# Row sums of a seven-product output projection made by accumulating DMAs instead of GpSimd, and squares of the other half's tokens at other heads

## The chip, the cores and the metric

The kernel runs on one core of a Trainium2 chip. Its engines are TensorE (PE in the profile; PEld is its weight load), VectorE (DVE), ScalarE (ACT), GpSimd (POOL) and SyncE (SP, which here only issues DMAs). Each works through its own queue in order. DMAs are issued from SP's queue (hardware_dynamic) and POOL's (software_dynamic). The metric is the device time of one execution in microseconds (us), as the median of several runs.

## The reference

One decoder layer over 1024 tokens of width 2048, in f32. Two groups of 8 heads share one input projection:

```python
hn = rmsnorm(h, norm_mix_g[i])
proj = hn @ w_in[i]
# heads 0-7: stick-breaking attention (products of 1 - sigmoid in place of a softmax)
# heads 8-15: differential attention (softmax1 - lam * softmax2), with its own RMSNorm
mixed = jnp.concatenate([sb_out * jax.nn.silu(sb_g), df_out * jax.nn.silu(df_g)], axis=-1)
h = h + mixed @ w_out[i]
gate = jax.nn.sigmoid(rmsnorm(h, norm_ple_g[i]) @ w_ple_gate[i])
h = h + gate * (p[i] @ w_ple_proj[i])
return rmsnorm(h, norm_final_g)
```

`mixed` is 1024 x 2048: sixteen head outputs of 128 columns.

## The kernel before, in words

Everything lies transposed: features on the 128 partitions, tokens along the row, reversed and in two halves of 512. Half 1, which holds the earlier tokens, is worked first, then half 0, whose attention also reads the keys and values of half 1. Each f32 matmul is made of three on float32r: every operand is split into a high part (a cast on ACT) and a low part (a difference on DVE), and high x high, high x low and low x high are summed in PSUM (L213 to L215).

**Input projection and attention.** For each half and each head, two units (`unit`) of 96 matmuls give q and k, then v and the gate. Their weights come as four blocks of 512 KB per unit: a load on SP (L150), the cast `whi` on ACT (L151) and the difference `wlo` on DVE (L152), each in two buffers. The attention of a head is a list of steps with due times. A counter goes up after every three matmuls, and a step that is due is put among the matmuls of the next head's units (`Side.tick`). PE's order is therefore written out by hand over the whole kernel. Up to the second output projection below, the other queues are ordered by a planner that simulates the program.

A step of a stick-breaking head: scores on PE, sigmoids on ACT (L304, L305), a running product (L306) and a product (L307) on DVE, transposes on PE (L345), splits (`lead` L350/L351, `awh`/`awl` L357/L358), and the product with v on PE (L373 to L378). DVE's instruction at L554 makes the gate's input and marks the start of each head's attention. The head's output is multiplied into the gate's tile `sg` (three buffers; L387 for stick-breaking, L408 for differential heads) and stored to DRAM as `mixed_d[half, head]` from SP (L389, L410). In half 1, k and v are also stored from POOL's queue; in half 0 they are loaded from there, again by POOL's queue, into `k2` and `v2`, two buffers each.

Half 1 runs heads 0 to 15. Half 0 runs 8 to 15 and then 0, 4, 1, 5, 2, 6, 3, 7.

**Squares.** The norm of the tokens of half 0 needs the sum of squares over 16 row blocks of x. At the ninth head of half 1 (`hd == H`), 16 loads (L585, the `xt` ring of four buffers, held back until the last weight load issued by then), 16 squares on ACT (L105, L109; two buffers `sq`) and 15 additions on POOL (L110) make it. It is used two heads later.

**Output projection.** It is made of two phases, each over eight heads as inner dimension: first heads 8 to 15, then 0 to 7. In each phase the 2 x 2 block product (two halves of tokens, two groups of four heads) takes seven block products in place of eight. With A11 and A12 the two groups of half 1, A21 and A22 those of half 0, the row sums are S1 = A21 + A22, S2 = S1 - A11, S3 = A21 - A11 and S4 = A12 - S2. `combine_` makes them, head pair by head pair: four loads of `mixed_d` on SP (L246), four additions or subtractions of 128x512 on POOL (L249 to L252) and four stores to `comb_d` on SP (L254). `combine` is called after a head of half 0 where a pair is complete, eight times in all, the last one in the middle of the first phase; it holds its loads until the last put before it, if there is one. Each sum is later loaded by SP and split by ACT and DVE (`load_operand`).

For the weights, DVE makes differences (`diff`) of four blocks; the fourth, `b22`, goes with S4. `whigh` casts each on ACT (L865) and `wlow` makes the low part on DVE (L876). The results go out through `put`, from POOL's queue: a plain store to `half_d` in the first phase (L746), an accumulating DMA into `h_d` in the second (L744). In this part DVE and ACT are ordered by hand too. The ring of `sg` is used again here for `u2` and `u3` (L965 and following).

After that come the gate's projection and the final norm.

Of the kernel before, what the change touches and what calls it, by code (L numbers as in the profile page):

```python
# [13 lines left out]
F32 = mybir.dt.float32  # L14
F32R = mybir.dt.float32r
BF16 = mybir.dt.bfloat16
AF = mybir.ActivationFunctionType
ALU = mybir.AluOpType
AX = mybir.AxisListType

P = 128
D = 2048
S = 1024
HALF = 512
NK = D // P
H = 8
SB_SCALE = 128.0 ** -0.5
DF_SCALE = 64.0 ** -0.5
ORDER1 = [*range(16)]
ORDER0 = [*range(8, 16), 0, 4, 1, 5, 2, 6, 3, 7]  # L30
EPS = 1e-6
SUB_EPS = 1e-5

# [13 lines left out]
def _body(ctx, nc, tc, ap):  # L47
# [4 lines left out]
    ev = ctx.enter_context(tc.tile_pool(name="ev", bufs=1))  # L52
    pp = ctx.enter_context(tc.tile_pool(name="pp", bufs=2, space=PSUM))
    dram = ctx.enter_context(tc.tile_pool(name="dram", bufs=1, space=bass.MemoryType.DRAM))
    V, G, A, T = nc.vector, nc.gpsimd, nc.scalar, nc.tensor
# [163 lines left out]
    mixed_d = dram.tile([2, NK, P, HALF], F32, name="mixed_d", tag="mixed_d")  # L219

    comb_d = dram.tile([2, 4, 4, P, HALF], F32, name="comb_d", tag="comb_d")
    h_d = dram.tile([2, NK, P, HALF], F32, name="h_d", tag="h_d")
    part_d = dram.tile([8, P, HALF], F32, name="part_d", tag="part_d")
    half_d = dram.tile([2, NK, P, HALF], F32, name="half_d", tag="half_d")
# [4 lines left out]

    KA = [[(8 + i, 12 + i) for i in range(4)], [(i, 4 + i) for i in range(4)]]  # L230

    def combine(ph, i):

        a, b = KA[ph][i]
        if lastput[0] is not None:
            with tc.issue_after(lastput[0].ins):
                return combine_(ph, i, a, b)
        return combine_(ph, i, a, b)

    lastput = [None]  # L240

    def combine_(ph, i, a, b):
        t = []
        for src in (mixed_d[0, a], mixed_d[0, b], mixed_d[1, a], mixed_d[1, b]):
            x = ev.tile([P, HALF], F32, name="cmb", tag="xt", bufs=4)
            nc.sync.dma_start(x, src)  # L246
            t.append(x)
        a21, a22, a11, a12 = t
        G.tensor_tensor(a22, a21, a22, op=ALU.add)  # L249
        G.tensor_tensor(a21, a21, a11, op=ALU.subtract)  # L250
        G.tensor_tensor(a11, a22, a11, op=ALU.subtract)
        G.tensor_tensor(a12, a12, a11, op=ALU.subtract)  # L252
        for j, x in enumerate((a22, a11, a21, a12)):
            nc.sync.dma_start(comb_d[ph, j, i], x)  # L254


    def attention(at, pz, half, hd, q, qz, K, KL, VV, sg, vf):
# [102 lines left out]
        def mix(pr, g):  # L360
            if g == 0:
                avs[pr] = pp.tile([P, 4, P], F32, name="av", tag="t")
            av4 = avs[pr]
            av = av4[:, 2:4, :].rearrange("p a b -> p (a b)")
            for j in range(2):
                blk = 2 * (pr + g) + j
                vv = VV[blk // 4]
                last = blk == nb - 1
                if blk == 2 * pr:


                    for i in range(2):
                        T.matmul(av4[:, 0:2, :], vv[:, i, blk % 4, :], wjs[pr, g][j], start=i == 0, stop=i == 1)  # L373
                    continue
                wh, wl = wjs[pr, g][j]
                T.matmul(av, vv[:, 0, blk % 4, :], wh, start=blk == 2 * pr + 1, stop=False)  # L376
                T.matmul(av, vv[:, 1, blk % 4, :], wh, start=False, stop=False)  # L377
                T.matmul(av, vv[:, 0, blk % 4, :], wl, start=False, stop=last)  # L378
            if not last:
                return  # L380
            ms_ = slice(pr * 2 * P, (pr + 1) * 2 * P)
            sm = ev.tile([P, 2, P], F32, name="sm", tag="sm", bufs=5)
            A.copy(sm[:, 1, :], av4[:, 3, :])
            V.reduce_sum(sm[:, 0, :], av4[:, 0:3, :].rearrange("p a b -> p b a"), axis=AX.X)
            av = sm.rearrange("p a b -> p (a b)")
            if sb:
                V.tensor_tensor(sg[:, ms_], av, sg[:, ms_], op=ALU.mult)  # L387
                if pr == 1:
                    nc.sync.dma_start(mixed_d[half, hd], sg)  # L389
                return  # L390
            sq = ev.tile([P, 2 * P], F32, name="sqv", tag="sm", bufs=5)
            A.activation(sq, av, AF.Square)
            V.scalar_tensor_tensor(sg[:, ms_], av, subg[:, 0:1], sg[:, ms_], op0=ALU.mult, op1=ALU.mult)
            sqh = ev.tile([P, 2 * P], F32R, name="sqh", tag="sm", bufs=5)
            sql = ev.tile([P, 2 * P], F32R, name="sql", tag="sm", bufs=5)
            A.copy(sqh, sq)
            V.tensor_tensor(sql, sq, sqh.bitcast(F32), op=ALU.subtract)
            sqs[pr] = sq, sqh, sql

        def norm(pr):  # L400
            ms_ = slice(pr * 2 * P, (pr + 1) * 2 * P)
            sq, sqh, sql = sqs[pr]
            msq = pp.tile([P, 2 * P], F32, name="msq", tag="t")
            T.matmul(msq, onesr, sqh, start=True, stop=False)
            T.matmul(msq, onesr, sql, start=False, stop=True)
            rs_ = ev.tile([P, 2 * P], F32, name="rsub", tag="sm", bufs=5)
            rstd_from(msq, 1.0, eps5, SUB_EPS, rs_, sq)
            V.tensor_tensor(sg[:, ms_], sg[:, ms_], rs_, op=ALU.mult)  # L408
            if pr == 1:
                nc.sync.dma_start(mixed_d[half, hd], sg)  # L410

        n0 = nb // 2
        n1 = n0 - 1
# [20 lines left out]
    with tc.tile_pool(name="at", bufs=2) as at, tc.tile_pool(name="pz", bufs=2, space=PSUM) as pz:  # L434
# [4 lines left out]
        for half in (1, 0):  # L439
            tsl = slice(half * HALF, half * HALF + HALF)  # L440
            X = {}
            if half == 1:
# [3 lines left out]
                for i in range(8):  # L446
# [4 lines left out]
                    src = ap["xT"].rearrange("(a k p) t -> k p a t", a=2, p=P)[kts[0], :, :, tsl]  # L451
# [9 lines left out]
                    for j in range(2):  # L461
                        kt = kts[j]
                        X[kt] = split_scaled(kt, x2[:, j, :], gvec[:, 0, kt:kt + 1])
                        xs.append(x2[:, j, :])
            else:
                for kt in KT:
                    xt = ev.tile([P, HALF], F32, name="xt", tag="xt", bufs=4)
# [5 lines left out]

            for hd in (ORDER0, ORDER1)[half]:
                sb = hd < H
# [79 lines left out]
                sg = at.tile([P, HALF], F32, name="sg", tag="sg", bufs=3)  # L555
# [20 lines left out]
                    K.append(k2)  # L576
                    VV.append(v2)
                side.add(attention(at, pz, half, hd, q, qz, K, KL, VV, sg, vf))
                if half == 1 and hd == H:
                    pin = lastw[0].ins  # L580
                    ss0 = SumSq(ev, "ssq")
                    for kt in range(NK):
                        xt = ev.tile([P, HALF], F32, name="xs", tag="xt", bufs=4)
                        with tc.issue_after(pin):
                            nc.sync.dma_start(xt, ap["xT"][kt * P:(kt + 1) * P, 0:HALF])  # L585
                        ss0.add(xt)
                if half == 1 and hd == H + 2:
                    rstds[0] = ss0.rstd(ev, "rstd0")
                if half == 0 and hd >= H:
                    for kt in (2 * (hd - H), 2 * (hd - H) + 1):  # L590
                        for hf in range(2):
                            with tc.issue_after(lastw[0].ins):
                                nc.sync.dma_start(h_d[hf, kt], ap["xT"][kt * P:(kt + 1) * P, hf * HALF:hf * HALF + HALF])
                if half == 0 and hd < H and hd:
                    n = ORDER0.index(hd) - H
                    combine(*((0, n - 1) if n < 5 else (1, n - 5)))


        h = {}
# [141 lines left out]
        def put(o, ph, hf, ch):  # L741

            if ph:
                lastput[0] = G.dma_start(h_d[hf, ch], o, accum_op=ALU.add)  # L744
            else:
                lastput[0] = G.dma_start(half_d[hf, ch], o)  # L746

        def ftile():
            return ev.tile([P, HALF], F32, name="hc", tag="f", bufs=4)
# [28 lines left out]
        for u in range(0, 8, 2):  # L778
# [8 lines left out]
            for i in range(2):  # L787
                product(u + i, 0, "A12", aa[i], False, tick=True)
                o = ftile()
# [64 lines left out]
        def whigh():  # L854
            i = len(wmade)
            if i == len(wtodo):
                return
            n, nm, fn = wtodo[i]
            src = fn()
            pool, tag = WRING[i % len(WRING)]  # L860
            if pool == "wp":
                t = wp.tile([P, 2, 4 * P], F32R, name="wpr", tag=tag)
            else:
                t = at.tile([P, 2, 4 * P], F32R, name="wpr", tag=tag, bufs=BUFS.get(tag, 2))
            A.copy(t[:, 0], src)  # L865
            wmade.append((src, t))

        def wlow():
            i = wlate[0]
            if i == len(wtodo):  # L870
                return
            wlate[0] += 1
            n, nm, _ = wtodo[i]
            src, t = wmade[i]
            wmade[i] = None
            V.tensor_tensor(t[:, 1], src, t[:, 0].bitcast(F32), op=ALU.subtract)  # L876
            ph, u = UNITS[n]
            wq[u, ph, nm] = t[:, 0], t[:, 1]
            if nm == "S4":
                wload(n + 2, 22)  # L880
# [61 lines left out]
        for ph in range(2):  # L942
            for u in range(8):
# [6 lines left out]
                if ph:  # L950
                    a = pp.tile([P, HALF], F32, name="pa", tag="acc", bufs=2)
# [6 lines left out]
                if ph == 0 and u % 3 == 2:  # L958
                    b, c = [pp.tile([P, HALF], F32, name="pb", tag="acc", bufs=2) for _ in range(2)]
                else:  # L960
                    bc = pz.tile([P, 2, HALF], F32, name="pbc", tag="z")
                    b, c = bc[:, 0, :], bc[:, 1, :]
# [29 lines left out]
                o = ftile()  # L992
# [4 lines left out]
                if last:  # L997
                    p2()
                prev = u, ph, b, c, s1, u2
                if ph == 0 and u == 1:  # L1000
                    combine(1, 3)
                if ph == 0 and 1 <= u < 5:
                    for nm, i in (("A11", u - 1), ("A12", u - 1)):
                        xq.append((slot[0] + 3, load_operand(1, nm, i)))
        ph = pair("ph", "k", F32R)
# [35 lines left out]
        ss0 = SumSq(ev, "rstd1")  # L1041
# [43 lines left out]
        for pc in range(4):  # L1085
            raw = wp.tile([P, 2, 2, 2, P], F32, name="wraw", tag="wraw", bufs=2)
            nc.sync.dma_start(raw, ap["w_gate"][7][pc])
            for k2 in range(2):
# [3 lines left out]
                else:  # L1092
                    t = pair(f"wz{kk}", H1[kk], F32R, (P, 2, 2, 2, P))
# [5 lines left out]
        for tq in range(2):  # L1099
# [13 lines left out]
            for c in range(2):  # L1113
                t = h[0, 7 + 8 * c][:, ts]
# [72 lines left out]
```

## Time and profile before

| | us |
|---|---|
| median of 3 runs | 2515.78 (2513.76 to 2515.96) |
| the profiled execution | 2510.27 |
| its span, first to last instruction | 2508.5 |
| PE busy | 2441.4 (97%) |
| DVE busy | 1668.4 (67%) |
| ACT busy | 1161.9 (46%) |
| POOL busy | 288.9 (12%) |

The first half of the tokens runs from 0 to about 860 us, the second to about 1765, the first phase of the output projection to about 1930 and the second to 2084, the gate and the end to 2508. A matmul of 512 columns takes some 390 ns in the records, but the next starts some 230 ns after it; busy time of PE is their union.

In a timeline, a line has the start and the duration in us, engine, line of the kernel and operation, what it writes and reads with the shape, and in brackets the idle time of the engine before it and what ended that. In a list of waits, the numbers are the total in us, how many times, and the longest. In a list of DMA issues, the last number is the median time in us from issue to landing.

### The profile page before, as it was taken

To read this page: it belongs to the slowest core of one execution; us is meant where nothing else is said; L and a number is where in the kernel's file an instruction comes from. 1 tells how busy PE (TensorE), PEld (TensorE's weight loads), DVE (VectorE), ACT (ScalarE), POOL (GpSimd) and SP (SyncE) were. 2 spreads that over 40 slices of the span, in tenths; PEclk is the share of its full clock that TensorE was granted. 3 is DMA by queue.
4 is the path that set the end of the run, shared out by engine and by line. 5 is a ranking of instruction groups with operands and counts; after the bars stand their busy time and mean duration, and the time that the engine had idled before them with its cause. 6 is when DMAs were issued, how large, how long until landed. Compare 5 with 4: busy or idle time off the path is not lost.

```text
span 2508.5 us, 31234 instructions
## 1 busy us (share of the span) xinstructions
PE 2441.4 (97%) x11626; PEld 2034.8 (81%) x11626; DVE 1668.4 (67%) x2677; ACT 1161.9 (46%) x1920; POOL 288.9 (12%) x281
## 2 busy tenths in 40 slices
PE   8999999999999999999999999999999998999996
PEld 7888888788887888888887888887787876888886
DVE  6554555777877888888876565667678673547555
ACT  6332333555556655555555333335523224637342
POOL 3000000300000000001111010101021114321112
PEclk9999999999999999999999999999999999999998
DMA  5333333633334333334443333435656786333433
GB/s 189 113 116 116 114 105 125 206 123 118 109 122 164 121 107 122 114 117 143 148 142 126 101 126 94 135 113 183 228 190 217 164 199 211 129 119 115 133 101 101
DMA packets 135415, 346.26 MB, mean 138 GB/s; under 512 B 14496, under 2 KB 18592, under 8 KB 135264
## 3 DMA queue, kind: packets, MB, share of 16 engines
q1 hardware_dynamic: 114096, 288.43, 35.6%
q0 software_dynamic: 21168, 55.85, 7.8%
q8 instruction: 91, 1.49, 0.2%
q14 instruction: 60, 0.49, 0.1%
HBM read 281.31 MB, written 71.30 MB: 141 GB/s over the span
## 4 chain that ended last, share of the span: by engine, by line
PE 87%; DVE 7%; DMA 2%; ACT 2%; issue 1%; SPq 0%; DVEq 0%; ACTq 0%
PE acc L213 20%; PE acc L214 20%; PE acc L215 20%; PE tp L345 2%; PE pbc L756 2%; PE pbc L758 2%; PE pbc L757 2%; DVE st L306 1%; PE z L286 1%; PE z L287 1%; PE av L378 1%; DVE wlo L152 1%; PE av L377 1%; PE av L376 1%; PE pa L758 1%
## 5 line engine op out<-in xcount | busy, mean ns | idle before, releaser
L213 PE MATMUL acc<-xh,whi 128*128 128x512 f32 x2464 | 981.4, 398 | 6.3 <-ACT xh L138 6.3
L214 PE MATMUL acc<-xl,whi 128*128 128x512 f32 x2464 | 963.9, 391 | 0.8 <-DVE xl L139 0.8
L215 PE MATMUL acc<-xh,wlo 128*128 128x512 f32 x2464 | 964.0, 391 | 0.0
L152 DVE TENSOR_TENSOR wlo<-wraw,whi 128x1024 fp32r<-128x1024 f32 (+1 forms) x317 | 398.8, 1258 | 374.5 <-ACT whi L151 369.2
L215 PEld LDWEIGHTS acc<-xh,wlo 128*128 128x128 f32 x2464 | 463.6, 188 | 101.1 <-DVE wlo L152 1.3
L151 ACT CAST whi<-wraw 128x1024 fp32r<-128x1024 f32 (+1 forms) x317 | 333.0, 1051 | 457.2 <-PE acc L214 397.0
L213 PEld LDWEIGHTS acc<-xh,whi 128*128 128x128 f32 x2464 | 464.8, 189 | 93.6 <-ACT xh L138 6.8
L214 PEld LDWEIGHTS acc<-xl,whi 128*128 128x128 f32 x2464 | 464.9, 189 | 88.3 <-DVE xl L139 2.3
L357 ACT CAST awh<-tp 128x256 fp32r<-128x256 f32 (+1 forms) x160 | 80.3, 502 | 180.9 <-PE tp L345 153.5
L358 DVE TENSOR_TENSOR awl<-tp,awh 128x256 fp32r<-128x256 f32 (+1 forms) x160 | 93.1, 582 | 97.9 <-ACT awh L357 96.7
L110 POOL TENSOR_TENSOR ssq<-ssq,sq 128x512 f32<-128x512 f32 x80 | 119.0, 1488 | 326.6 <-ACT sq L109 278.8
L314 ACT ACTIVATE et<-z,mx 128x512 f32<-128x512 f32 (+7 forms) x128 | 94.6, 739 | 53.6 <-DVE mx L311 52.7
L865 ACT CAST wpr<-T 128x512 fp32r<-128x512 f32 x64 | 39.2, 623 | 164.9 <-DVE T L822 164.0
L306 DVE TENSOR_TENSOR_SCAN st<-pt 128x511 f32<-128x511 f32 (+3 forms) x64 | 89.9, 1405 | 20.8 <-ACT pt L304 20.2
L311 DVE TENSOR_REDUCE mx<-z 128x1 f32<-128x512 f32 (+7 forms) x128 | 96.4, 753 | 1.2
L304 ACT ACTIVATE pt<-z 128x512 f32<-128x512 f32 (+3 forms) x64 | 41.6, 650 | 79.7 <-DVE z L293 79.7
L378 PE MATMUL av<-awl,v 128*128 128x256 f32 x256 | 73.4, 287 | 5.2 <-DVE awl L358 5.2
L376 PE MATMUL av<-awh,v 128*128 128x256 f32 x256 | 72.5, 283 | 0.7 <-ACT awh L357 0.7
L377 PE MATMUL av<-awh,v 128*128 128x256 f32 x256 | 72.3, 283 | 0.0
L286 PE MATMUL z<-k,q 128*128 128x512 f32 (+2 forms) x160 | 56.9, 360 | 4.5 <-ACT et L314 4.5
L322 DVE SCALAR_TENSOR_TENSOR et<-et,l 128x512 f32<-128x512 f32 (+3 forms) x64 | 53.0, 829 | 11.8 <-ACT et L321 11.8
L321 ACT ACTIVATE et<-et,l 128x512 f32<-128x512 f32 (+3 forms) x64 | 49.7, 777 | 17.6 <-DVE l L320 17.1
(309 smaller groups left out, 3627.8 us busy)
## 6 DMA issues: line engine op xcount, KB each, us to landing
wraw<-w_in SPq DMA_DIRECT2D x255, 512.0 KB, 3.6
wraw<-w_gate SPq DMA_DIRECT2D x64, 512.0 KB, 3.6
wraw<-w_out SPq DMA_DIRECT2D x56, 256.0 KB, 3.7
k_d<-k POOLq DMA_DIRECT2D x16, 512.0 KB, 3.9
v_d<-v POOLq DMA_DIRECT2D x16, 512.0 KB, 2.9
mixed_d<-sg SPq DMA_DIRECT2D x32, 256.0 KB, 3.1
k<-k_d POOLq DMA_DIRECT2D x16, 512.0 KB, 3.6
v<-v_d POOLq DMA_DIRECT2D x16, 512.0 KB, 4.4
```

The lines of the kernel that those rows point to most:

```text
L110: lastadd[0] = eng.tensor_tensor(self.acc, self.acc, s, op=ALU.add)
L151: A.copy(hi[:, o], raw[:, o])
L152: V.tensor_tensor(lo[:, o], raw[:, o], hi[:, o].bitcast(F32), op=ALU.subtract)
L213: T.matmul(acc[c], hi[:, k2, kh, c, :], xh, start=first, stop=False)
L214: T.matmul(acc[c], hi[:, k2, kh, c, :], xl, start=False, stop=False)
L215: T.matmul(acc[c], lo[:, k2, kh, c, :], xh, start=False, stop=last)
L306: V.tensor_tensor_scan(st[:, off + 1:nkey], pt[:, off:nkey - 1], pt[:, off:nkey - 1], initial=1.0, op0=ALU.mult, op1=ALU.bypass)
L311: V.reduce_max(mx, z[:, vw], axis=AX.X, negate=True)
L314: A.activation(et[:, vw], z[:, vw], AF.Exp, bias=mx[:, 0:1], accum_out=l)
L376: T.matmul(av, vv[:, 0, blk % 4, :], wh, start=blk == 2 * pr + 1, stop=False)
L377: T.matmul(av, vv[:, 1, blk % 4, :], wh, start=False, stop=False)
L378: T.matmul(av, vv[:, 0, blk % 4, :], wl, start=False, stop=last)
```

## The change

`combine` goes. Each head's output is added to the row sums that it is part of as soon as it is there, by a new function `mixed` in place of the store:

- Half 1, a first-group head (A11): `mixed_d` is stored as before; ACT makes a negated copy in a tile of the `xt` ring, and three plain stores on SP put it into S2, S3 and S4.
- Half 1, a second-group head (A12): `mixed_d` as before; the negated copy is added to S4 by one accumulating DMA from POOL's queue.
- Half 0, a first-group head (A21): no store to `mixed_d`; the tile is stored to S1 from SP and added to S3, S2 and S4 by three accumulating DMAs.
- Half 0, a second-group head (A22): `mixed_d` from SP; the tile is added to S1, S2 and S4 by three accumulating DMAs.

S4 so comes out with the opposite sign, and the weights that go with it are negated in their split. Half 0 now runs its stick-breaking heads in the order 0 to 7. The squares are made four blocks at a time at heads 1 to 4 of half 1. The holding of `combine` behind the last put goes with it.

```diff
-ORDER0 = [*range(8, 16), 0, 4, 1, 5, 2, 6, 3, 7]
+ORDER0 = [*range(8, 16), *range(8)]
...
-    def combine_(ph, i, a, b):
-        t = []
-        for src in (mixed_d[0, a], mixed_d[0, b], mixed_d[1, a], mixed_d[1, b]):
-            x = ev.tile([P, HALF], F32, name="cmb", tag="xt", bufs=4)
-            nc.sync.dma_start(x, src)
-            t.append(x)
-        a21, a22, a11, a12 = t
-        G.tensor_tensor(a22, a21, a22, op=ALU.add)
-        G.tensor_tensor(a21, a21, a11, op=ALU.subtract)
-        G.tensor_tensor(a11, a22, a11, op=ALU.subtract)
-        G.tensor_tensor(a12, a12, a11, op=ALU.subtract)
-        for j, x in enumerate((a22, a11, a21, a12)):
-            nc.sync.dma_start(comb_d[ph, j, i], x)
+    def mixed(half, hd, t):
+
+
+        ph, second, i = (0 if hd >= H else 1), hd % H >= 4, hd % 4
+        S1, S2, S3, S4 = [comb_d[ph, j, i] for j in range(4)]
+        if half == 1 or second:
+            nc.sync.dma_start(mixed_d[half, hd], t)
+        if half == 1:
+            n = ev.tile([P, HALF], F32, name="neg", tag="xt", bufs=4)
+            A.activation(n, t, AF.Copy, scale=-1.0)
+            if second:
+                G.dma_start(S4, n, accum_op=ALU.add)
+            else:
+                for d in (S2, S3, S4):
+                    nc.sync.dma_start(d, n)
+            return
+        if second:
+            G.dma_start(S1, t, accum_op=ALU.add)
+        else:
+            nc.sync.dma_start(S1, t)
+            G.dma_start(S3, t, accum_op=ALU.add)
+        G.dma_start(S2, t, accum_op=ALU.add)
+        G.dma_start(S4, t, accum_op=ALU.add)
...
                 if pr == 1:
-                    nc.sync.dma_start(mixed_d[half, hd], sg)
+                    mixed(half, hd, sg)
...
-                if half == 1 and hd == H:
+                if half == 1 and 1 <= hd < 5:
                     pin = lastw[0].ins
-                    ss0 = SumSq(ev, "ssq")
-                    for kt in range(NK):
+                    if hd == 1:
+                        ss0 = SumSq(ev, "ssq")
+                    for kt in range(4 * hd - 4, 4 * hd):
                         xt = ev.tile([P, HALF], F32, name="xs", tag="xt", bufs=4)
                         with tc.issue_after(pin):
                             nc.sync.dma_start(xt, ap["xT"][kt * P:(kt + 1) * P, 0:HALF])
...
-                if half == 0 and hd < H and hd:
-                    n = ORDER0.index(hd) - H
-                    combine(*((0, n - 1) if n < 5 else (1, n - 5)))
...
-            A.copy(t[:, 0], src)
+            if nm == "S4":
+                A.activation(t[:, 0], src, AF.Copy, scale=-1.0)
+            else:
+                A.copy(t[:, 0], src)
...
-            V.tensor_tensor(t[:, 1], src, t[:, 0].bitcast(F32), op=ALU.subtract)
+            if nm == "S4":
+                V.scalar_tensor_tensor(t[:, 1], src, -1.0, t[:, 0].bitcast(F32), op0=ALU.mult, op1=ALU.subtract)
+            else:
+                V.tensor_tensor(t[:, 1], src, t[:, 0].bitcast(F32), op=ALU.subtract)
...
-                if ph == 0 and u == 1:
-                    combine(1, 3)
```

More of the change, by code (lines that the diff above doesn't have):

```diff
@@ L230, in _body @@
     KA = [[(8 + i, 12 + i) for i in range(4)], [(i, 4 + i) for i in range(4)]]
[L232 to L240, printed above, removed]
-    def combine_(ph, i, a, b):
-        t = []
-        for src in (mixed_d[0, a], mixed_d[0, b], mixed_d[1, a], mixed_d[1, b]):
-            x = ev.tile([P, HALF], F32, name="cmb", tag="xt", bufs=4)
-            nc.sync.dma_start(x, src)
-            t.append(x)
-        a21, a22, a11, a12 = t
[L249 to L252, printed above, removed]
-        for j, x in enumerate((a22, a11, a21, a12)):
-            nc.sync.dma_start(comb_d[ph, j, i], x)
+    def mixed(half, hd, t):
[19 more added lines that the diff above has]
+        G.dma_start(S4, t, accum_op=ALU.add)
     def attention(at, pz, half, hd, q, qz, K, KL, VV, sg, vf):
@@ L409, in norm @@
             if pr == 1:
-                nc.sync.dma_start(mixed_d[half, hd], sg)
+                mixed(half, hd, sg)
         n0 = nb // 2
@@ L743, in put @@
             if ph:
-                lastput[0] = G.dma_start(h_d[hf, ch], o, accum_op=ALU.add)
+                G.dma_start(h_d[hf, ch], o, accum_op=ALU.add)
             else:
-                lastput[0] = G.dma_start(half_d[hf, ch], o)
+                G.dma_start(half_d[hf, ch], o)
         def ftile():
```

## The prediction

> **What bounds the kernel now.** I read the page's busy times first, then who TensorE (PE) waits for, then the timelines of VectorE (DVE), GpSimd (POOL) and ScalarE (ACT) around those waits.
>
> ```profile
> span 2508.5 us, 31234 instructions
> ...
> PE 2441.4 (97%) x11626; PEld 2034.8 (81%) x11626; DVE 1668.4 (67%) x2677; ACT 1161.9 (46%) x1920; POOL 288.9 (12%) x281
> ...
> PE 87%; DVE 7%; DMA 2%; ACT 2%; issue 1%; SPq 0%; DVEq 0%; ACTq 0%
> ```
>
> PE carries 87% of the chain that ended last, and the diff leaves its matmuls as they are. So the change can only open or close waits of PE, of which the profile shows 67 us (2508.5 - 2441.4). The waits of PE by line put these first inside attention:
>
> ```profile
> PE av L373 <- DVE lead L351: 5.4, 5, 1.6
> PE av L378 <- DVE awl L358: 5.2, 7, 0.9
> ...
> PE z L286 <- ACT et L314: 4.5, 2, 3.5
> ```
>
> The next question is what makes DVE late. The timeline of DVE has one instruction per head that marks the step (L554). Four stick-breaking heads of the second half in a row:
>
> ```profile
> 1397.79 0.69 DVE L554 TENSOR_TENSOR gf<-acc,rstd 128x512 f32<-128x512 f32 x1 [2.03 <-PE acc L215]
> ...
> 1454.26 0.69 DVE L554 TENSOR_TENSOR gf<-acc,rstd 128x512 f32<-128x512 f32 x1 [2.03 <-PE acc L215]
> ...
> 1513.90 0.69 DVE L554 TENSOR_TENSOR gf<-acc,rstd 128x512 f32<-128x512 f32 x1 [2.03 <-PE acc L215]
> ...
> 1570.36 0.69 DVE L554 TENSOR_TENSOR gf<-acc,rstd 128x512 f32<-128x512 f32 x1 [2.03 <-PE acc L215]
> ```
>
> The periods are 56.47, 59.64 and 56.46 us: every second head is 3.17 us longer. POOL's timeline has one set of the four sums of `combine_` in exactly the long ones:
>
> ```profile
> 1459.08 2.54 POOL L249 TENSOR_TENSOR cmb<-cmb 128x512 f32<-128x512 f32 x1 [8.14 <-DMA cmb<-mixed_d]
> 1461.70 2.16 POOL L250 TENSOR_TENSOR cmb<-cmb 128x512 f32<-128x512 f32 x1
> 1463.93 2.88 POOL L251 TENSOR_TENSOR cmb<-cmb 128x512 f32<-128x512 f32 x1
> 1466.89 2.02 POOL L252 TENSOR_TENSOR cmb<-cmb 128x512 f32<-128x512 f32 x1
> ```
>
> And DVE does the same product of 128x1023 in the short head (first line) and beside these sums (second):
>
> ```profile
> 1404.18 1.23 DVE L307 TENSOR_TENSOR bt<-st,bt 128x1023 f32<-128x1023 f32 x1
> ...
> 1460.64 2.06 DVE L307 TENSOR_TENSOR bt<-st,bt 128x1023 f32<-128x1023 f32 x1
> ```
>
> Sums on POOL slow DVE, the transposes' input comes late, and PE waits 1.6 us at L373 and 0.6 at L378, among others.
>
> **The change part by part.** The profiled execution took 2510.27 us (span 2508.5 and 1.8 around it), 5.5 us below the median of 2515.78 (2513.76 to 2515.96). I sum against 2510.27 and add the 5.5 again.
>
> *POOL's sums go.* 32 additions (16.4 + 14.3 + 14.2 + 14.1 = 59 us of POOL) leave. In time: sets in the three stick-breaking heads that start at 1454, 1570 and 1686 give back 3.17 us each, 9.5. The set at 1183 to 1190 falls in a differential head of 60.48 us and that at 1244 in one of 60.51, where those before take 58.49: 4.0. The set at 1304 falls in a period of 58.63 (0.1, left out), the one at 1366 in the first stick-breaking period, 62.67, whose stalls (at 1342 and 1357) precede the set: between 0 and 2.0, I take 0. The last, at 1833, has no PE wait beside it: 0. Sum 13.5; from 10 to 15.5.
>
> *The squares (L585).* 16 loads on SP, 16 squares on ACT and 15 additions on POOL leave head 8 of the first half. There they stand ahead of the gate and the table load:
>
> ```profile
> 449.33 0.64 ACT L109 ACTIVATE sq<-xs 128x512 f32<-128x512 f32 x1 [1.71 <-DMA xs<-xT]
> 450.20 0.64 ACT L109 ACTIVATE sq<-xs 128x512 f32<-128x512 f32 x1 [0.23 <-POOL ssq L110]
> 450.74 1.04 ACT L151 CAST whi<-wraw 128x1024 fp32r<-128x1024 f32 x1
> 451.68 0.63 ACT L109 ACTIVATE sq<-xs 128x512 f32<-128x512 f32 x1
> 452.21 0.62 ACT L557 ACTIVATE sg<-gf 128x512 f32<-128x512 f32 x1
> 452.84 1.28 ACT L482 ACT_TABLE_LOAD   x1
> ```
>
> PE waits 3.5 us for the exponential behind this (L286 on L314). Three squares are 1.9 us of ACT, and beside the additions DVE's L152 takes 2.18 for 1.23 and L562 1.55 for 0.69, 1.8 more. The table load stays. I take 3.0 of 0 to 3.6.
>
> They come back four per head in heads 1 to 4. If they cost as much there as a set of `combine_`, 3.17 x 4 = 12.7. But in that half the product of the second row block ends at 207.8 and ACT then waits 4.06 us for the transposes (L350, at 213.90): some 5 us of room against 3.3 us of slowing, and the periods are 48.99 from head 2 to head 7. An addition queued behind POOL's store of v (it waits 26.5 us for its input) could hold the third square through the two `sq` buffers; ACT is 32% busy there (47.6 of 150 us), so that stays short. I take 0 of 0 to 12.7.
>
> *SP.* 64 issues go (loads and stores of `combine_`), 8 stores of `mixed_d` go, 24 stores of the negated tile and 8 of S1 come: 96 become 56. SP waits 5 us at a time for L152 to free a weight buffer, and the casts of weights wait for PE (397 us) but 2.1 us for their load. A store that waits for the negated copy holds the next weight load by as much; it starts about 8 us before it is needed too late: loaded by 241.55 + 3.6 = 245.2, cast at 250.0 (room 4.9), needed a quarter unit later (5.4 less 2.3 of cast and difference, 3.1). 0.
>
> *ACT.* 16 negated copies of 128x512 in the first half at 0.72 us (as L138): 11.5 us of ACT, after each head's output. In the head shown the output is ready at 236.4 and ACT is free from 234.4 to 239.2. 0, at most 11.5. The S4 copies with a scale are 0.72 for 0.62 and DVE's form with a scalar 0.70 for 0.69, on engines with idle time: 0.
>
> *POOL's 56 accumulating DMAs.* Their nearest rows are the puts of the second phase, beside the plain puts of the first:
>
> ```profile
> half_d<-hc POOLq DMA_DIRECT2D x32, 256.0 KB, 3.5
> ...
> h_d<-hc POOLq DMA_DIRECT2D x32, 256.0 KB, 5.1
> ```
>
> Each holds POOL 0.86 us (0.54 plain): 48 us for the 59 removed. Three per head follow an output of the second half. They stand before loads of k and v that have a whole head in hand. The tile `sg` is held longer, but has three buffers: a period of 56 us or more is left against 2.6 of issue and 6.8 of the longest landing. Only at the end is it tight: the last output is stored at 1804.0, and the third use of that ring by the next part is at 1820.2 (L965). Behind the put at 1819.3 instead, the last three would land at about 1829: 0 to 9 us, I take 0, since their input is ready 15 us earlier. No accumulation is needed soon: the second phase loads S1 to S4 from 1899 on.
>
> On the DMA engines: from 1850 to 1930 a share of 0.63 moved 207 GB/s (3.0 us per MB), from 1931 to 2084 0.78 moved 186. With 32 accumulations (55 GB/s) taken out, the rest costs 0.40, which leaves 0.38 x 153 / 32 = 1.8 us each (estimate), against 0.8 for a plain one. Three are 5.4 us, inside the weights' 8. [...]
>
> *Head order.* 0, 4, 1, 5 becomes 0, 1, 2, 3: same shapes, 0.
>
> Sum: -13.5 - 3.0 = -16.5. 2510.27 - 16.5 = 2493.8, and 5.5 more is 2499.3.
>
> **The rivals.**
> (a) The additions cost in heads 1 to 4 what they cost in the second half: -16.5 + 12.7 = -3.8, 2512.0. For it: the slowing of DVE. Against: the 5 us of room.
> (b) Issuing an accumulation holds DVE as a sum does. A set holds POOL 7.2 us for 3.17 lost; three issues are 2.6, so 1.15 per head and 18 over 16 heads: 2517.7. Against: from 1931 to 2084 DVE's steps of 128x512 stay at 0.68 to 0.70 beside issues of 0.85 to 0.90. [...]
> (c) Slower: the three accumulations of a second-half head delay weights. It decides where the burst passes 8 us. At twice my estimate it is 10.8, 2.8 late in 16 heads, +45: 2544. For it: landings up to 6.8 us. Against: 5.4 and a page with no PE wait for a load.
> (d) DVE, ACT, POOL and SP are ordered by a planner up to 1800 us, and a new order opens waits like those at 1342 and 1357 (3.9 together) at four places: 2515, no change.
>
> **How the numbers follow.** Forecast 0.71, its own range 2494 to 2506 (full gains with the open 2.0 and 0.6 below; half of (a) above). (a) 0.07, (b) 0.05, (c) 0.09, (d) 0.08. A difference under 0.2% (5 us) can't be told from none. Faster: the forecast and half of (a), 0.74. Same: the rest of (a), (b) and most of (d), 0.14. Slower: (c) and the rest, 0.12. The range takes in (a) and stops short of (b): 2494 to 2514.
>
> **What would show it.** Right: periods of 56.5 in all stick-breaking heads of the second half but the first and last, and of 58.5 in the differential ones; L307 of 128x1023 at 1.23; no PE wait at 453; periods of 49.0 in heads 1 to 4 though L152 is slowed there. Wrong: waits of the weight casts for their loads, periods above 49 in heads 1 to 4, or DVE waiting for a `sg` buffer after 1804.

## The result, and the profile after

| us | before | after |
|---|---|---|
| median of 4 runs each | 2514.77 (2513.39 to 2515.96) | 2501.69 (2495.95 to 2502.27) |
| the profiled execution, its span | 2510.27, 2508.5 | 2502.27, 2500.5 |

The ratio is 0.9937, with a 95% interval of 0.9923 to 0.9951: 0.6% faster. Six more runs of the changed kernel, told of below, had a median of 2496.51. Over all ten it is 2497.5 (2493.79 to 2503.28), against 2499.3 forecast.

The page of the changed kernel first (span; busy times; shares of the chain that ended last):

```profile
span 2500.5 us, 31265 instructions
...
PE 2441.6 (98%) x11626; PEld 2037.5 (81%) x11626; DVE 1645.0 (66%) x2677; ACT 1169.3 (47%) x1936; POOL 280.5 (11%) x305
...
PE 90%; DVE 4%; DMA 3%; ACT 1%; issue 1%; POOL 0%; SPq 0%; DVEq 0%; ACTq 0%
```

PE's busy time has not moved (2441.4 before), DVE's has fallen by 23 us, and PE carries 90% of the chain instead of 87%. Then the waits of PE by line, after (in the order of the list):

```profile
PE av L378 <- DVE awl L358: 1.6, 2, 0.8
...
PE z L286 <- ACT et L314: 1.1, 1, 1.1
...
PE av L373 <- DVE lead L351: 0.8, 2, 0.5
```

These three were 5.2, 4.5 and 5.4. The timeline of DVE in the stick-breaking heads of the second half, after:

```profile
1443.22 0.69 DVE L554 TENSOR_TENSOR gf<-acc,rstd 128x512 f32<-128x512 f32 x1 [2.03 <-PE acc L215]
...
1449.60 1.23 DVE L307 TENSOR_TENSOR bt<-st,bt 128x1023 f32<-128x1023 f32 x1
...
1499.68 0.69 DVE L554 TENSOR_TENSOR gf<-acc,rstd 128x512 f32<-128x512 f32 x1 [2.03 <-PE acc L215]
```

The product takes 1.23 us where it took 2.06 beside the sums, and the period is 56.46 where this head had 59.64. The timeline of ACT where the squares stood, at the ninth head of the first half (`hd` 8 in the kernel), after:

```profile
450.76 1.05 ACT L151 CAST whi<-wraw 128x1024 fp32r<-128x1024 f32 x1 [4.34 <-PE acc L214]
451.72 0.62 ACT L557 ACTIVATE sg<-gf 128x512 f32<-128x512 f32 x1
452.36 1.28 ACT L482 ACT_TABLE_LOAD   x1
454.50 0.69 ACT L314 ACTIVATE et<-z,mx 128x512 f32<-128x512 f32 x1 [0.86 <-DVE mx L311]
```

The gate and the table load follow the cast at once.

Put one under the other, the starts of the heads (L554) in the two profiled executions give this account. Heads are counted from 1 in it; `hd` is one less. The rows behind the last head come from the starts of PE's matmuls; `za` is what the second unit of the gate's projection writes.

| place (time after, us) | after minus before, us |
|---|---|
| before the first head's L554 (57) | +2.1 |
| head 4 of the first half | +0.3 |
| period of head 9 there, behind the squares: 55.24 to 49.87 | -5.4 |
| periods of heads 15 and 16: 59.03 to 55.52, 50.50 to 50.08 | -3.9 |
| differential heads with a set of sums: 60.48, 60.51, 58.63 to 58.49 | -4.1 |
| stick-breaking heads with a set: 59.64, 59.63, 60.89 to 56.47, 56.47, 57.74 | -9.5 |
| sum at the last head's L554: 1747.35 to 1726.83 | -20.5 |
| from there to the first matmul into `za`: 362.67 to 375.49 | +12.8 |
| from there to the end: 398.49 to 398.18 | -0.3 |
| span | -8.0 |

So 20.5 us were gained by the last head, more than the 16.5 forecast, and most of the gain was given back behind it. Two rows stand in no forecast and come in part from these two executions. At the start, 14 matmuls run at half rate after and 4 before (0.2 us lost by each, as worked out in the last section). In head 15, PE waits 3.3 us at L345 before and 1.8 after, and a stretch at half clock stands behind it before alone.

Behind the last head's L554, the accumulating DMAs of the last two heads are issued. The timeline of POOL, after:

```profile
1726.60 0.86 POOL L249 DMA_DIRECT2D comb_d<-sg  x1 [57.04 <-DVE sg L387]
1727.14 1.22 POOL L253 DMA_DIRECT2D comb_d<-sg  x1
1727.68 1.58 POOL L254 DMA_DIRECT2D comb_d<-sg  x1
...
1788.89 0.88 POOL L249 DMA_DIRECT2D comb_d<-sg  x1 [9.26 <-DVE sg L387]
1789.46 1.21 POOL L253 DMA_DIRECT2D comb_d<-sg  x1
1790.02 1.54 POOL L254 DMA_DIRECT2D comb_d<-sg  x1
```

Behind each burst ACT or DVE waits for a load longer than before. The timelines of ACT (the split of S4) and DVE (a difference of weights), after:

```profile
1733.92 0.62 ACT L726 CAST cS4h<-cS4l 128x512 fp32r<-128x512 f32 x1 [3.05 <-DMA cS4l<-comb_d]
```
```profile
1801.22 0.69 DVE L820 TENSOR_TENSOR T<-wraw 128x512 f32<-128x512 f32 x1 [5.70 <-DMA wraw<-w_out]
```

and the same two places before:

```profile
1751.69 0.62 ACT L728 CAST cS4h<-cS4l 128x512 fp32r<-128x512 f32 x1 [0.47 <-DMA cS4l<-comb_d]
```
```profile
1813.19 0.69 DVE L822 TENSOR_TENSOR T<-wraw 128x512 f32<-128x512 f32 x1 [2.28 <-DMA wraw<-w_out]
```

The slowest of the four loads of S4 took 7.1 us from issue to landing where the fastest took 4.3; the slowest weight took 7.9 where the median was 4.3. PE then waits in turn: behind the first burst for `bt` (L305), which stands behind the late split in ACT's queue, and behind the second for `wpr`, which is made from the late weights. Of its waits from 1720 to 1830 us, after, these three have no counterpart in the list of before:

```profile
PE pbc L754 <- ACT wpr L866: 2.0, 1, 2.0
...
PE z L282 <- ACT bt L305: 1.3, 1, 1.3
PE pbc L756 <- DVE wpr L880: 1.1, 1, 1.1
```

And in both executions there are stretches of some microseconds in which PE, though busy, runs at half the clock. In windows of the trace (busy us and instructions of PE, PEld, DVE, ACT, POOL; granted clock; DMA share; GB/s), after, such a stretch and the one that follows it:

```profile
1748.00:1752.50 4.50, 4.50 (x11) 3.53 (x12) 1.60 (x3) 0.37 (x1) 0.52 (x1) 0.50 0.71 228
1752.50:1757.00 4.50, 4.50 (x24) 3.94 (x23) 0.69 (x1) 1.34 (x3) 0.00 (x0) 0.92 0.51 195
```

11 matmuls against 24 in the same time. The execution before has one right behind the wait for the squares, and a long one in head 15:

```profile
457.80:460.00 2.20, 2.20 (x7) 1.79 (x6) 1.82 (x5) 1.92 (x6) 1.62 (x2) 0.50 0.45 160
```
```profile
800.00:805.00 5.00, 5.00 (x14) 3.84 (x13) 4.31 (x8) 2.17 (x5) 0.00 (x0) 0.50 1.07 324
```

Theory: the sums and the squares are worth what the account says, and the two last bursts take back part of it by delaying loads. Rivals: the head order or another side effect loses it; or the loss is the chance of these two executions.

### The profile page after: what moved, and what is told of

Same layout as the page of the kernel before. It is cut to its first block, busy times and chain, and to the rows that moved or that the text cites. A ratio compares the mean times of both kernels' runs of the same rounds, so it can differ in the third digit from the quotient of the medians.

```text
span 2500.5 us, 31265 instructions
## 1 busy us (share of the span) xinstructions
PE 2441.6 (98%) x11626; PEld 2037.5 (81%) x11626; DVE 1645.0 (66%) x2677; ACT 1169.3 (47%) x1936; POOL 280.5 (11%) x305
## 4 chain that ended last, share of the span: by engine, by line
PE 90%; DVE 4%; DMA 3%; ACT 1%; issue 1%; POOL 0%; SPq 0%; DVEq 0%; ACTq 0%
PE acc L213 22%; PE acc L214 21%; PE acc L215 21%; PE tp L345 2%; PE pbc L754 2%; PE pbc L756 2%; PE pbc L755 2%; PE z L287 1%; PE z L286 1%; PE av L378 1%; PE av L377 1%; PE av L376 1%; PE pa L756 1%; PE pa L754 1%; PE pa L755 1%
## 5 line engine op out<-in xcount | busy, mean ns | idle before, releaser
L152 DVE TENSOR_TENSOR wlo<-wraw,whi 128x1024 fp32r<-128x1024 f32 (+1 forms) x317 | 395.5, 1248 | 377.0 <-ACT whi L151 372.2
L286 PE MATMUL z<-k,q 128*128 128x512 f32 (+2 forms) x160 | 56.6, 358 | 1.1 <-ACT et L314 1.1
L287 PE MATMUL z<-kl,qz 128*128 128x512 f32 (+2 forms) x160 | 57.5, 359 | 0.0
```

The source lines that it names most:

```text
L152: V.tensor_tensor(lo[:, o], raw[:, o], hi[:, o].bitcast(F32), op=ALU.subtract)
```

## The experiments

**The squares alone, and all but the squares.** First the changed kernel with the squares back at `hd` 8:

```diff
-                if half == 1 and 1 <= hd < 5:
+                if half == 1 and hd == H:
                     pin = lastw[0].ins
-                    if hd == 1:
-                        ss0 = SumSq(ev, "ssq")
-                    for kt in range(4 * hd - 4, 4 * hd):
+                    ss0 = SumSq(ev, "ssq")
+                    for kt in range(NK):
```

> The changed kernel with the squares back at head 8 (16 loads, 16 squares, 15 additions there, none at heads 1 to 4); the row sums stay with the DMAs. If the squares ahead of the gate caused the wait of PE at head 9, the period of that head is again about 55.2 us (49.9 in the changed kernel), PE waits some 3.5 us for the exponential there, and the kernel is 3 to 6 us slower than the changed one: 2505 to 2508 where the kernel before takes 2515. Rival: the wait comes from the table load alone, then the period stays near 50 and the time near 2502. The periods of the second half (58.49 and 56.47) must not change in either case.

Measured: 2504.8 (2504.26 to 2509.68), ratio to before 0.9967 (0.9954 to 0.998). That is 3.1 above the first median of the changed kernel and 7.3 above that of its ten runs. The period of head 9 is 56.18, those of the second half stay at 58.49 and 56.47. The wait is back (list of PE's waits), behind the same queue on ACT (timeline):

```profile
PE z L286 <- ACT et L314: 6.5, 2, 4.5
```
```profile
453.94 0.63 ACT L109 ACTIVATE sq<-xs 128x512 f32<-128x512 f32 x1 [0.73 <-POOL ssq L110]
454.48 1.04 ACT L151 CAST whi<-wraw 128x1024 fp32r<-128x1024 f32 x1
455.43 0.62 ACT L109 ACTIVATE sq<-xs 128x512 f32<-128x512 f32 x1
455.95 0.61 ACT L557 ACTIVATE sg<-gf 128x512 f32<-128x512 f32 x1
```

The other way round, the kernel before with its squares at `hd` 1 to 4 (the same edit reversed):

> The kernel before with only the squares moved to heads 1 to 4; sums stay on GpSimd. Theory: head 9 at about 50 us in place of 55.2, the long periods 60.5 and 59.6 stay, the time is 3 to 6 us under the kernel before (ratio 0.9976 to 0.9988). Rival (a): the additions beside heads 1 to 4 cost there, periods above 49.0 in heads 1 to 4 and a ratio of 1.000 or more.

Measured: 2508.87 (2506.71 to 2510.58), ratio 0.9974 (0.9962 to 0.9985): 5.2 us below the 2514.02 of before measured beside it, within the 3 to 6 expected. What is left of the wait of L286 stands in head 15 (list of PE's waits):

```profile
PE z L286 <- ACT et L314: 1.7, 1, 1.7
```

The period of head 9 is 49.87, and the periods of the heads that take the squares stay at 48.37 to 49.02. The long periods of the second half stay. So the squares are worth 5 us where 3.0 had been forecast. The starts of PE's matmuls say why, for the profiled execution before: 3.6 us go in the wait of L286 (3.86 from one start to the next in place of 0.23), and 1.6 more in the slow matmuls of the half-clock stretch behind it. In the copy with the squares back there is one at 461.7 to 464.6 too. The wait had been sized at 3.0 of 0 to 3.6; the stretch behind it was not in the sum. Some of the 5.2 may also come from head 15, whose wait at L345 is 1.9 here and 3.3 before; the squares alone do not set it, since it is 1.8 with the squares back as well.

**The sums alone.** The kernel before, with its loads and stores, without the four additions:

```diff
-        G.tensor_tensor(a22, a21, a22, op=ALU.add)
-        G.tensor_tensor(a21, a21, a11, op=ALU.subtract)
-        G.tensor_tensor(a11, a22, a11, op=ALU.subtract)
-        G.tensor_tensor(a12, a12, a11, op=ALU.subtract)
```

> The kernel before with the four additions and subtractions of each set on GpSimd left out; the loads from mixed_d and the stores to comb_d stay, so that S1 to S4 hold unsummed tiles. Theory (GpSimd's additions slow VectorE): the periods of 60.5 become 58.5 and those of 59.6 become 56.5, 13.5 us less up to the end of attention, and a ratio of about 0.9946. Rival: the long periods come from the loads and stores of the sets, or from the head order; then they stay at 60.5 and 59.6 and the ratio is 1.000.

Measured: 2500.36 (2499.76 to 2502.74), ratio 0.9944 (0.9929 to 0.9958), 13.7 us below before. The differential periods are 58.49, the stick-breaking ones 56.47 to 56.75, and the product beside which a sum stood takes 1.22 (timeline of DVE, four lines of the file earlier):

```profile
1507.40 0.69 DVE L550 TENSOR_TENSOR gf<-acc,rstd 128x512 f32<-128x512 f32 x1 [2.03 <-PE acc L215]
...
1513.78 1.22 DVE L303 TENSOR_TENSOR bt<-st,bt 128x1023 f32<-128x1023 f32 x1
```

The loads and stores of `combine_` cost nothing that shows; the additions were the cost, 13.5 by the forecast.

**The last six accumulations.** The changed kernel with those of `hd` 6 and 7 of the second half left out:

```diff
+        if hd in (6, 7):
+            return
         if second:
             G.dma_start(S1, t, accum_op=ALU.add)
```

> The changed kernel without the six accumulating DMAs of the last two heads of half 0 (heads 6 and 7), so that S1, S2 and S4 lack these tiles. Theory: the two bursts delay the load of cS4l (7.1 us to landing in the changed kernel, 4.3 before) and two loads of the projection's weights (7.9 and 7.6 against 4.5), and PE loses 2.7 us at 1734, 2 us more at half clock behind it and 6 us at 1801. Without them these loads land in 4 to 5.6 us and the kernel takes 8 to 12 us less than the changed one: ratio 0.989 to 0.991. Rival: the loss there comes from the changed order of the queues; then the ratio stays at 0.994.

Measured: 2494.73 (2491.97 to 2494.79), ratio 0.9921 (0.9906 to 0.9936), a smaller gain than the 0.989 to 0.991 expected. All 56 accumulations as plain stores, so that the last store wins:

```diff
-            G.dma_start(S1, t, accum_op=ALU.add)
+            G.dma_start(S1, t)
...
-        G.dma_start(S2, t, accum_op=ALU.add)
-        G.dma_start(S4, t, accum_op=ALU.add)
+        G.dma_start(S2, t)
+        G.dma_start(S4, t)
```

> The changed kernel with all 56 accumulating DMAs of the heads as plain stores of the same size from the same queue, so that the last store wins in place of the sum. If reading and adding in the DMA is what delays the neighbours, the burst takes about 3 x 0.8 us of the engines in place of 3 x 1.8, cS4l and the weights land within 5.5 us, and half or more of the 10 us comes back: ratio 0.990 to 0.992. If three transfers in a row do it whatever they are, the landings stay above 7 us and the ratio is 0.994.

Measured: 2495.85 (2494.24 to 2499.5), ratio 0.9926 (0.9909 to 0.9942), between the two expectations. Its issues hold POOL less (timeline):

```profile
1789.14 0.54 POOL L249 DMA_DIRECT2D comb_d<-sg  x1 [9.25 <-DVE sg L387]
1789.68 0.54 POOL L253 DMA_DIRECT2D comb_d<-sg  x1
1790.21 0.54 POOL L254 DMA_DIRECT2D comb_d<-sg  x1
```

DVE's wait for `wraw` (4.8) and the longest landing of S4 (6.4) shrink but stay. Then a version that computes everything, with those six issued from a copy loaded back inside the first phase:

```diff
+        if hd in (6, 7):
+            late.extend((hd, d) for d in (S1, S2, S4))
+            return
...
+                if ph == 0 and 2 <= u < 4:
+                    hd = late[0][0]
+                    lt = ev.tile([P, HALF], F32, name="lt", tag="xt", bufs=4)
+                    nc.sync.dma_start(lt, mixed_d[0, hd])
+                    for _ in range(3):
+                        G.dma_start(late.pop(0)[1], lt, accum_op=ALU.add)
```

> The changed kernel with the six accumulations of heads 6 and 7 made later, at the third and fourth unit of the first phase, from tiles loaded back from mixed_d. The result is the full one. Theory: there the weights are loaded a unit (13 us) ahead and the bursts cost nothing, so the time is that of the kernel without them, ratio 0.989 to 0.991. Rival: the bursts delay weights wherever they stand; then the loss moves to about 1840 and the ratio stays near 0.994.

Measured: 2492.82 (2491.22 to 2493.81), ratio 0.9915 (0.99 to 0.993). The ratio is just above the 0.989 to 0.991 expected. The six were not moved as far as meant: the reloads are issued early (from 1730.9), and POOL's timeline has the bursts only 8 us later than in the changed kernel:

```profile
1734.62 2.67 POOL L1014 DMA_DIRECT2D comb_d<-lt  x3 [64.65 <-DMA lt<-mixed_d]
...
1797.06 2.66 POOL L1014 DMA_DIRECT2D comb_d<-lt  x3 [6.44 <-DMA lt<-mixed_d]
```

That is behind the four loads of S4, and behind the first four of the weight loads that stood beside the second burst (issued from 1791.4 to 1796.5). What waited for `wraw` from 1780 to 1830 (tile view), with the landing times of these loads, in this version:

```profile
  DVE T L825: 2.5, 1
...
DMA to landing us min/median/max: 3.2/4.3/6.0
```

**The head order.** The changed kernel with the order 0, 4, 1, 5, 2, 6, 3, 7:

```diff
-ORDER0 = [*range(8, 16), *range(8)]
+ORDER0 = [*range(8, 16), 0, 4, 1, 5, 2, 6, 3, 7]
```

> The changed kernel with the old head order 0, 4, 1, 5, 2, 6, 3, 7 in half 0. The order was priced at 0: periods of 56.47 in all stick-breaking heads but the first and last, and a time within 3 us of the changed kernel. If the order matters, a period differs.

Measured, a single run: 2499.79. The periods of the second half and the waits are those of the changed kernel (5.9 for `wraw`); the order is worth nothing that can be seen, and the loss is there without it.

**How much of the loss is chance.** The changed kernel and the later version again, six executions of each on one chip:

> The changed kernel once more, beside the version in which the last six accumulations come later, on the same chip. Theory (the two last bursts of three accumulations cost 2.7 + 6.3 us by the timelines, some of it covered): this kernel is 6 to 10 us slower than that version, near 2500. Rival (the earlier executions of this kernel, 2495.95 to 2502.27, were high by chance, by stretches of half clock rather than by waits for loads): the difference is under 4 us, and the two ranges overlap.

> The same version as the one with the last six accumulations later, again, beside the changed kernel. In its profile those six were issued only some 8 us later than in the changed kernel (at 1734.6 and 1797.1 against 1726.6 and 1788.9), behind the loads of S4 and behind two of the weight loads. Theory: 2492 to 2495, 6 to 10 below the changed kernel, with no wait of DVE for wraw above 3 us near 1800 and none of ACT for cS4l above 1.5 us. Rival: under 4 us below.

Measured: the changed kernel 2496.51 (2493.79 to 2503.28, six runs; ratio 0.993, 0.9912 to 0.9948), the later version 2494.65 (2493.49 to 2497.55, six; ratio 0.9921, 0.9907 to 0.9936). The difference is 1.9 us and the ranges overlap: the 6 to 10 us of the theory fell. The later version still had a wait of 4.2 us for `wraw` in its second profile, against the 3 expected at most. The tile view of `wraw` in the changed kernel, second profile:

```profile
  DVE T L820: 7.1, 1
...
DMA to landing us min/median/max: 2.6/4.1/8.2
```

So the wait behind the second burst is there again, and longer. But S4 waited no longer here than before (1.7 us against 1.6; its loads landed within 4.7), and the stretch that ran at half clock in the first profile ran at full clock here:

```profile
1748.00:1752.50 4.50, 4.50 (x27) 3.89 (x26) 0.69 (x1) 1.31 (x3) 0.00 (x0) 1.00 0.82 319
```

The stretch near 1748 is not the bursts' either: the versions without the last six and with them later have one there too, of nine matmuls each, like the first profile of the changed kernel.

All profiles beside each other, by DVE's wait for `wraw` near 1800, by PE's waits for `wpr` there (from 1720 to 1850), by the matmuls at half rate right behind (all of those from 1770 to 2050), and by the time from the last head's L554 to the first matmul into `za`, which takes in every loss of the end:

| kernel | DVE's wait for `wraw`, us | PE's for `wpr`, us | half-rate matmuls | last head to `za`, us |
|---|---|---|---|---|
| before; without the sums; squares moved alone | 2.3; 2.4; 2.5 | 0; 0; 0.2 | 0; 0; 0 | 362.7; 364.9; 368.4 |
| last six accumulations left out | 2.6 | 0.3 | 0 | 366.8 |
| last six later, twice | 2.5, 4.2 | 0.2, 1.6 | 0, 7 | 366.9, 369.4 |
| all as plain stores | 4.8 | 2.2 | 6 | 372.2 |
| old head order | 5.9 | 2.8 | 10 | 374.5 |
| squares back | 5.5 | 2.9 | 0 | 371.8 |
| changed kernel, twice | 5.7, 7.1 | 3.1, 4.5 | 12, 5 | 375.5, 371.3 |

The two groups, with three transfers at once in their place and without or later, do not overlap in either wait or in the time (371.3 us and up, 369.4 and down); plain stores lie with the first. The waits grow in the order none or later (2.3 to 4.2 us for DVE, 0 to 1.6 for PE), plain (4.8 and 2.2), accumulating (5.5 to 7.1 and 2.8 to 4.5). So the bursts delay loads, mostly because they are three transfers at once; that accumulating adds to it rests on the one profile of the plain stores. In time it is less than one profile suggested: ten runs of the changed kernel have a median of 2497.5, ten of the later version 2493.9, 3.6 us apart (in 87 of the 100 pairs the later version is faster; the runs are from several chips on which before had 2514.3 to 2515.3, and on the one chip that ran both the 1.9 is not clear of their spread). So the size is 2 to 4 us and not known better.

Of the 12.8, 6.8 stand right behind the bursts in the first profile: 4.4 of waits (the three lines above) and 2.4 in the 12 matmuls at half rate behind the second. In the second profile it is 5.5 (4.5 and 1.0), in the later version 0.2 and 3.0. The rest is in no line of the bursts and goes with the spread between executions: the end of before's profile was the shortest of its group by 2 to 7 us, with 6 matmuls at half rate in it where the others of the group have 14 to 21, and its whole execution lay 4.5 below its median.

## Why the prediction was right

The direction, its mechanism and the time (2499.3 against 2501.69, and 2497.5 over ten runs) held; that the time came so close is partly luck, as the sum at the end shows. Step by step:

- **POOL's sums, -13.5.** Held, period for period: 4.1 in the differential heads and 9.5 in the stick-breaking ones by the account, 13.7 as a time when the additions alone are left out. The 2.0 left open at the first stick-breaking period are not there (62.67 in both).
- **The squares, -3.0 of 0 to 3.6.** Mis-sized: 5.2 alone. The wait itself was 3.6, and 1.6 us of half clock follow it; that stretch was in no term.
- **The additions in heads 1 to 4, 0 of 0 to 12.7.** Held: periods of 48.99, with 0.3 more in one, though L152 takes 1.55 to 2.23 beside them instead of 1.22. Rival (a) falls.
- **Issues of accumulations and DVE.** Rival (b) falls. While the three issues of 0.86 to 1.58 us run at 1726.6 to 1729.3, DVE's operations of 128x512 take 0.68 to 0.69. (This rival was priced with 7.2 us of POOL for a set; the set shown beside the long head holds it for 9.6, from 2.54 + 2.16 + 2.88 + 2.02.)
- **The negated copies, the stores on SP, the head order, 0.** Held. A copy took 0.63 us, not 0.72, and no wait of PE stands behind it.
- **"Three are 5.4 us, inside the weights' 8", 0.** This step failed, at two of the sixteen heads. The landings are 4.9, 7.1 and 8.3 us (medians by line, L249, L253 and L254, which are issued in this order), and the room of 8 us was read from the steady weight loads of attention. The loads of S4 and of the output projection's weights, at the last two heads, have less: DVE waited 2.3 us for such a weight in the kernel before already. That is rival (c) in small: 2 to 4 us in the medians in place of 45, since the periods of the other fourteen heads show no loss.
- **"Only at the end is it tight ... I take 0."** The place was right and the object wrong: nothing waits for `sg` after 1804; it is loads near 1734 and 1801 that are late.
- **Forecasting the median as profile plus 5.5.** The profiled execution after lies at its own median, so profile against profile is only -8.0, while the medians lie 13.1 apart in the first measurement and 18.8 in the last. The 2493.8 forecast for the profile was 8.5 too low for the first one and 2.4 for the second (2496.2).

In sum: -13.7 - 5.2 + 3.6 = -15.3, by the parts measured apart, against -16.5 forecast; two errors of 2 to 4 us, of opposite sign, are in it, and that they nearly cancel is luck. The later version has the lowest median of the three, 2493.9 over ten runs, against 2514.3 to 2515.3 for before and 2497.5 for the changed kernel.

## What to carry to other kernels

Additions that stand on an idle engine are not free if they slow another engine that feeds the matmuls (here DVE's product took 2.06 us beside POOL's sums and 1.23 without them, and the period was 59.64 in place of 56.47); the period of a repeated stage, with and without them, prices them to a tenth of a microsecond. Before work is moved onto DMAs, look for the load with the least room at each place where a burst is issued, above all where one stage changes into the next, and not at the room of the steady state. One profile against one profile can be wrong by several microseconds here: an account of losses needs a second profile of the same kernel before a mechanism is given the whole of it. And a late engine is a loss only where PE waits behind it: here PE's own waits and the half-rate matmuls behind them say how much.

## What the runs showed of the hardware that was not expected

In a half-clock stretch, matmuls of 512 columns start 0.427 us apart instead of 0.227, 3 to 13 of them in a row (1.3 to 5.6 us), with a granted clock of 0.50 in the windows shown above; beside the ten at 11.6 us in the profile after, the window from 11 to 16 us gives 1.00. That is 0.2 us per matmul, 2.6 for the thirteen of the longest, and in all eleven profiles the stretches stand at or right behind waits of PE, some behind waits of no more than 0.4 and 0.8 us (ahead of 434). But the same waits don't always bring one: before 1748, PE waited 2.0 and 0.9 us at L754 and L756 in the first profile of the changed kernel, and 1.7 and 1.1 in the second, and only the first has the stretch. They are a part of the spread between executions. Of the two profiles of the later version, the one with a stretch at 434 to 438 has a period of 52.93 for the eighth head of the first half, the one without it 51.34; the other nine profiles are 52.9 to 53.0 with such a stretch there (three) and 51.3 without (six). That they make most of the spread is argued from this, not shown.

In windows of the profiles of before and after, the granted clock is 0.50 for some 3.4 us at a time (from 456.9 and 2119.2 before, from 2111.6 after) or some 6.8 (from 798.3 and 2074.9 before, from 1746.4, 1804.4 and 2067.2 after), and for the last 17 us of both. The single waits ahead of a stretch can be much shorter than that (2.0 us at most ahead of 1748).

Accumulating DMAs issued back to back start 0.54 us apart, as plain ones do, but their records run on and overlap: 0.86, 1.22 and 1.58 us, so that three take POOL 2.7 us (1726.60 to 1729.26) and three plain ones 1.6. A plain put issued right behind the second burst (1790.56) took 1.56 too, where puts alone take 0.54 to 0.57.
